# Turning attention probabilities with VectorE's 32x32 transposes and SBUF block copies instead of TensorE transposes

## The chip, the cores and the metric

The kernel runs on one core of one Trainium2 chip. The metric is the device time of one execution in microseconds (us). Of the kernel before, three timed runs and one profiled execution exist.

## The reference

Two layers of a diffusion backbone work on 512 latent tokens and 256 context tokens of width 1024, in fp32. Layer 0 is differential attention with 8 heads (two softmaxes per head, the second subtracted with a factor), layer 1 is grouped-query attention with 8 query heads and 2 key/value heads. Cut to what matters here:

```python
s = jnp.einsum('bqhgd,bkhd->bhgqk', qblk, k32) * scale
p = jax.nn.softmax(s, axis=-1)
out = jnp.einsum('bhgqk,bkhd->bqhgd', p, v)
# latent queries read 512 latent and 256 context keys in one softmax;
# context queries (layer 0 only) read the 256 context keys
o = o1 - lam * o2                      # layer 0
y = (o * silu(gate)) @ w_out           # then x + gate * rms_norm(y)
```

The order of the keys in the sum over k is free, as long as the probabilities and the value tokens have the same one.

## The kernel before, in words

Every product of two fp32 matrices is done as three products of fp32r parts (`mm3`, line 537): high by high, high by low, low by high. A "split" of a tile is therefore a ScalarE copy to the high part and a subtraction on VectorE or GpSimd for the low part. Weights come from HBM 512 KB at a time on SP's DMA queue into two `raw` buffers and are split into `whi` and `wlo` (`wsplit`, line 606).

**Attention.** A unit is one block of 128 queries of one head. TensorE writes its scores, 128 queries by 768 keys, into PSUM (`s_units`, line 1264, layer 0; `s1_units`, line 1849, layer 1). VectorE takes the row maximum, ScalarE the exponential with the row sum, VectorE the reciprocal, and GpSimd scales the row; in layer 0 a VectorE multiply-add joins the second softmax to the first. The probabilities p then stand with the queries on the partitions, but the product with the values needs the keys there. `tstep` (line 1346 and line 1879) turns them: for two units (256 queries) and two key blocks, four TensorE transposes of 128x128 against `ident` go into one PSUM bank `bk`, which is split into `ah` (ScalarE) and `al` (VectorE). `mstep` (line 1360 and line 1892) multiplies with the value tiles in `pv_mm` (line 542): six matmuls with 256 columns per step. Three such steps make up a pair of units with 768 keys. Context queries in layer 0 have one step, with 256 keys.

**Projections.** `proj_fm` makes queries, keys and gates with the weights as the stationary operand. The values are made with the tokens as the stationary operand: `v_mm` (line 1038, layer 0) and `proj_tok` (line 1560, layer 1) load 128 token columns of `hhi`/`hlo` (or `h1hi`/`h1lo`) and stream 256 weight columns. Six token tiles, eight k-blocks and three products make 144 matmuls for a pair of heads; layer 0 has four pairs, layer 1 one.

**What sets the order.** The program is recorded and put in order before it is emitted. `Step` and `flow` (lines 731 and 746) set the order of recording: a score step has a due time, a turning step comes `LA` = 7.0 units of TensorE work after its last score step, and the product `LM` = 4.5 after the turning step; projections fill in between (`piece`, line 711). `Plan.schedule` (line 290) then replays all instructions with prices of its own (`price`, line 238) on the five in-order queues, and whichever can start first goes first. At most eight DMAs are taken to be in flight. Its result is the order of the instructions on each engine; the hardware only waits on semaphores. `AB` is the number of buffers of `ah` and of `al`.

Of the kernel before, what the change touches and what calls it, by code (L numbers as in the profile page):

```python
# [15 lines left out]
P = 128  # L16
# [31 lines left out]
WBUFS = 3  # L48
XE = [2, 2, 2, 2, 3, 3]
# [24 lines left out]
AB = 3  # L74
MEM = 227168
AHEAD_OPS = 1500
MARGIN = 1.08
SLOT = {}
# [400 lines left out]
def tile_backbone(  # L479
# [56 lines left out]

    def mm3(o, ahi, alo, bhi, blo, start, stop):
# [4 lines left out]
    def pv_mm(o, vh, vl, c, ah, al, kt, first, last):  # L542
        terms = [(v, a, e) for v, a in ((vh, ah), (vl, ah), (vh, al)) for e in range(2)]
        for i, (v, a, e) in enumerate(terms):
            nc.tensor.matmul(o, v[:, kt + e, c], a[:, e * 256:e * 256 + 256], start=first and i == 0, stop=last and i == 5)
# [577 lines left out]
    with pl.pool("t0") as t0:  # L1123
# [58 lines left out]
        def qk_split_(h, rr, eng=nc.gpsimd):  # L1182
            qk[h] = tuple(t0.tile([P, T], F32R, tag=f"qk{i}", name=nm("qk"), bufs=1) for i in range(4))
            for r, hi, lo in ((rr[0], *qk[h][:2]), (rr[1], *qk[h][2:])):
                nc.scalar.copy(hi, r)
                eng.tensor_tensor(lo, r, f32(hi), ALU.subtract)
# [77 lines left out]
        def s_units(h, qts):  # L1264
            res = []

            def unit(qt):
                k0, nk = (0, T) if qt < NQ else (512, C)
                l, ps_ = small(2), []
                if nk == T:  # L1270
                    sc = [sc2(), sc2()]
                else:
                    if h < KT - 1 or qt == NQ:
                        sts["sc"] = sc2()
                    sc = [sts["sc"]] * 2
                w = 384 if nk == T else 256
                qh, ql, kh_, kl_ = qk[h]
                tok = slice(qt * P, (qt + 1) * P)
                prev = None
                for j in range(nk // w):  # L1280
                    c = slice(k0 + j * w, k0 + j * w + w)
                    for i, (a, b) in enumerate(((qh, kh_), (qh, kl_), (ql, kh_))):
                        for m in (1, 0):
                            r = slice(m * 64, m * 64 + 64)
                            with after(prev), chained(prev):
                                prev = nc.tensor.matmul(
                                    sc[m][:, j if nk == T else m, :w], a[r, tok], b[r, c], start=i == 0, stop=i == 2)
                for m in range(2):
                    scv = sc[m][:, :, :384] if nk == T else sc[m][:, m, :256]
                    mx = small()  # L1290
                    nc.vector.tensor_reduce(mx, scv, AX.XY if nk == T else AX.X, ALU.max, negate=True)
                    pt = t0.tile([P, T], F32, tag=f"p{m}", name=nm("p"), bufs=6 if m == 0 else 2)[:, :nk]
                    pv_ = pt.rearrange("p (j n) -> p j n", j=2) if nk == T else pt
                    nc.scalar.activation(pv_, scv, AF.Exp, bias=mx, accum_out=l[:, m:m + 1])
                    ps_.append(pt)
                    r = l[:, m:m + 1]
                    nc.vector.reciprocal(r, r)
                    if m == 0:
                        scaled(EP0, pt, pt, r)
                    else:  # L1300
                        nc.vector.tensor_tensor(r, r, nlam, ALU.mult)
                        nc.vector.scalar_tensor_tensor(ps_[0], pt, r, ps_[0], ALU.mult, ALU.add)
                        res.append(ps_[0])

            def unit_ctx():
# [3 lines left out]
                for qt in (NQ, NQ + 1):  # L1309
                    tok = slice(qt * P, (qt + 1) * P)  # L1310
                    for i, (a, b) in enumerate(((qh, kh_), (qh, kl_), (ql, kh_))):
                        for m in (1, 0):
                            r = slice(m * 64, m * 64 + 64)
                            with after(prev), chained(prev):
                                prev = nc.tensor.matmul(
                                    sc[m][:, qt - NQ, :C], a[r, tok], b[r, S:T], start=i == 0, stop=i == 2)
                l = [small(2), small(2)]
                pts = []
                for m in range(2):
                    mx = small(2)  # L1320
                    nc.vector.tensor_reduce(mx, sc[m][:, :, :C], AX.X, ALU.max, negate=True)
                    pt = t0.tile([P, T], F32, tag=f"p{m}", name=nm("p"), bufs=6 if m == 0 else 2)
# [19 lines left out]
        def pv_steps(h, at, ch, after, ts, ms):  # L1342
            kts = range(6) if ch < 2 else range(4, 6)
            st = {}

            def tstep(kt):
                tr = trp()
                for e in range(2):
                    j = kt + e - kts[0]
                    for i, a in enumerate(at):  # L1350
                        nc.tensor.transpose(tr[:, e * 256 + i * P:e * 256 + (i + 1) * P], a[:, j * P:(j + 1) * P], ident)
# [4 lines left out]
                nc.scalar.copy(ah, tr)  # L1356
                nc.vector.tensor_tensor(al, tr, f32(ah), ALU.subtract)
                st[kt] = ah, al

            def mstep(kt):  # L1360
# [6 lines left out]
                pv_mm(o, vh, vl, vc, ah, al, kt, kt == kts[0], kt == kts[-2])  # L1367
                if kt == kts[-2]:
# [5 lines left out]
                    nc.scalar.copy(gT[h][:, sl], o)  # L1374
# [185 lines left out]
    def proj_tok(o, w, t):  # L1560
        sl = slice(t * P, (t + 1) * P)
        for kt in range(KT):
            wh, wl = w[kt // 4]
            c = slice((kt % 4) * 256, (kt % 4) * 256 + 256)
            mm3(o, h1hi[:, kt, sl], h1lo[:, kt, sl], wh[:, c], wl[:, c], kt == 0, kt == KT - 1)
# [127 lines left out]
    with pl.pool("t1", "right") as t1p:  # L1693
# [45 lines left out]
        def k_tr(m, kr):  # L1739
# [4 lines left out]
            sl = slice(m * P, (m + 1) * P)  # L1744
            nc.scalar.copy(kh[:, :, sl], tv)
            nc.vector.tensor_tensor(kl[:, :, sl], tv, f32(kh[:, :, sl]), ALU.subtract)

        def k_rope(m, o, r):
            kn = t1p.tile([P, 256], F32, tag="qt", name=nm("kn"), bufs=10)
# [4 lines left out]
            if m < NQ:  # L1754
                kr = t1p.tile([P, 256], F32, tag="qt", name=nm("kr"), bufs=10)
# [6 lines left out]
        for what, m in KV:  # L1762
# [7 lines left out]
            else:  # L1770
# [3 lines left out]
                run(proj_tok(o, wk if what == "k" else wv, m))  # L1774
# [21 lines left out]
        def q_proj(p):  # L1796
# [4 lines left out]
            for m in range(NQ):  # L1801
# [3 lines left out]
                q = t1p.tile([P, 256], F32, tag="qt", name=nm("q"), bufs=10)  # L1805
# [43 lines left out]
        def s1_units(h, ms):  # L1849
            res = []  # L1850

            def unit(m):
# [4 lines left out]
                for j in range(2):  # L1857
                    c = slice(j * 384, j * 384 + 384)
                    mm3(sc[:, j, :384], qa[:, sl], qb[:, sl], kh[:, g, c], kl[:, g, c], True, True)
# [6 lines left out]
                pt = t1q.tile([P, T], F32, tag="p", name=nm("p"), bufs=5)  # L1866
                l = small()
                nc.scalar.activation(pt.rearrange("p (j n) -> p j n", j=2), scv, AF.Exp, scale=sr, bias=nmx, accum_out=l)
                nc.vector.reciprocal(l, l)
                scaled(EN1, pt, pt, l)  # L1870
                res.append(pt)
# [3 lines left out]
        def pv1_steps(h, at, ch, after, ts, ms):  # L1875
            g = h // 4
            st = {}

            def tstep(kt):
                tr = trp()  # L1880
                for e in range(2):
                    for i, a in enumerate(at):
                        nc.tensor.transpose(tr[:, e * 256 + i * P:e * 256 + (i + 1) * P], a[:, (kt + e) * P:(kt + e + 1) * P], ident)
# [4 lines left out]
                nc.scalar.copy(ah, tr)  # L1888
                nc.vector.tensor_tensor(al, tr, f32(ah), ALU.subtract)
                st[kt] = ah, al  # L1890

            def mstep(kt):
# [5 lines left out]
                pv_mm(o, vh, vl, c, ah, al, kt, kt == 0, kt == 4)  # L1898
                if kt == 4:
                    if ch == 0:  # L1900
                        gT1[h] = t1p.tile([P, 512], F32, tag="g1", name=nm("g1"), bufs=8)
                    (nc.scalar.copy if EG1 == "a" else nc.vector.tensor_copy)(gT1[h][:, ch * 256:ch * 256 + 256], o)
# [217 lines left out]
```

## Time and profile before

| | us |
|---|---|
| timed runs, median of 3 (lowest, highest) | 807.85 (807.48, 809.25) |
| the profiled execution, its own time | 808.79 |
| span from its first to its last instruction | 807.0 |
| TensorE busy | 786.4 |
| VectorE / ScalarE / GpSimd busy | 473.6 / 482.0 / 437.4 |

PE stands for TensorE's matmuls, PEld for its weight loads, DVE for VectorE, ACT for ScalarE, POOL for GpSimd, SP for the engine whose queue issues most DMAs; a trailing q (SPq, ACTq) is a sequencer. A row of a group gives engine, operation, output <- inputs, shape and count, then the busy time and the mean duration of one in ns, then the idle time ahead of them. A row of the timeline gives the start, the length, and what ran; neighbours of one kind are merged (x4). Matmuls overlap: each has a duration of 270 to 400 ns, and the next one starts long before that is over, so the distance between ends is what one costs. The recorder writes every instruction with line 395, so groups are told apart by tile names: in `bk<-ident,p` the moving operand is `ident` and the loaded one is p.

### The profile page before, as it was taken

The numbers are of one execution on the slowest core, as the hardware profiler recorded it, in microseconds if no ns is written. First come the engines' busy times: TensorE is split into PE (matmuls) and PEld (weight loads), VectorE is DVE, ScalarE is ACT, GpSimd is POOL, SyncE is SP. The second block draws the span as 40 slices with busy tenths as digits, with TensorE's granted clock in tenths as the row PEclk, the third lists the DMA queues.
The fourth block names the chain that finished last, engine by engine and source line by source line (L and its number), as shares of the span: only waits on it lengthen the run. The fifth ranks groups of instructions, "written<-read, shape, count | busy, mean of one in ns | idle before, by whom it ended". The sixth has DMA issues, their size and how long they took to land.

```text
span 807.0 us, 14385 instructions
## 1 busy us (share of the span) xinstructions
PE 786.4 (97%) x5482; PEld 699.8 (87%) x5482; DVE 473.6 (59%) x824; ACT 482.0 (60%) x1083; POOL 437.4 (54%) x512
## 2 busy tenths in 40 slices
PE   7899999999999999999999999999999999999997
PEld 5779888889887898797989998898999899898886
DVE  3425787774847546656546743788346455655625
ACT  5524577684565645666538843784466676768622
POOL 4545776874585654757923312366887646644101
PEclk9899999999999999999999999999999999999999
DMA  9951120132142431323430152035321200201112
GB/s 302 363 180 67 65 75 31 40 108 89 40 158 79 144 105 53 105 80 96 165 106 27 62 227 79 1 89 175 120 70 53 96 11 27 79 27 55 51 53 105
DMA packets 41541, 77.78 MB, mean 96 GB/s; under 512 B 3584, under 2 KB 18688, under 8 KB 41472
## 3 DMA queue, kind: packets, MB, share of 16 engines
q1 hardware_dynamic: 38048, 71.71, 27.4%
q10 hardware_dynamic: 3424, 5.15, 1.8%
q8 instruction: 43, 0.70, 0.4%
q14 instruction: 26, 0.21, 0.1%
HBM read 70.56 MB, written 2.10 MB: 90 GB/s over the span
## 4 chain that ended last, share of the span: by engine, by line
PE 91%; DVE 3%; ACT 2%; DMA 2%; issue 1%; SPq 0%; POOL 0%; ACTq 0%; DVEq 0%; POOLq 0%
PE bk L395 75%; PE sc L395 16%; DMA ag<-in_ada_w 1%; DMA raw<-in_post_g 1%; DVE gacc L395 1%; DMA gw<-in_ada_w 0%; ACT whi L395 0%; SPq L395 0%; DVE h L395 0%; ACT sq L395 0%; DVE hf L395 0%; ACT p L395 0%; DVE sw L395 0%; DVE gate L395 0%; ACT jk L395 0%
## 5 line engine op out<-in xcount | busy, mean ns | idle before, releaser
L395 PE MATMUL bk<-whi,h 128*128 128x256 f32 (+1 forms) x1184 | 244.6, 299 | 2.0 <-DVE kn L395 1.3
L395 PE MATMUL bk<-h,whi 128*128 128x512 f32 (+2 forms) x832 | 225.6, 351 | 0.0
L395 POOL TENSOR_TENSOR wlo<-raw,whi 128x256 fp32r<-128x256 f32 x200 | 162.5, 839 | 76.7 <-ACT whi L395 75.3
L395 PEld LDWEIGHTS bk<-whi,h 128*128 128x128 f32 x1184 | 191.0, 189 | 14.6 <-issue 4.9
L395 PE MATMUL bk<-wlo,h 128*128 128x256 f32 (+1 forms) x592 | 176.5, 299 | 0.0
L395 PEld LDWEIGHTS bk<-h,whi 128*128 128x128 f32 x832 | 144.1, 188 | 16.5 <-issue 4.4
L395 PE MATMUL bk<-h,wlo 128*128 128x512 f32 (+2 forms) x416 | 145.7, 351 | 0.0
L395 DVE TENSOR_REDUCE sm<-sc 128x1 f32<-128x768 f32 (+2 forms) x114 | 101.0, 897 | 25.7 <-PE sc L395 25.4
L395 PEld LDWEIGHTS bk<-wlo,h 128*128 128x128 f32 x592 | 111.7, 189 | 4.8 <-issue 1.4
L395 POOL TENSOR_SCALAR p<-p,sm 128x768 f32<-128x768 f32 (+1 forms) x80 | 68.4, 858 | 77.6 <-DVE sm L395 72.8
L395 DVE TENSOR_TENSOR al<-bk,ah 128x512 fp32r<-128x512 f32 x104 | 69.4, 685 | 39.3 <-ACT ah L395 38.8
L395 ACT CAST whi<-raw 128x1024 fp32r<-128x1024 f32 (+1 forms) x70 | 71.7, 1026 | 31.9 <-PE bk L395 27.7
L395 ACT ACTIVATE p<-sc,sm 128x768 f32<-128x768 f32 (+1 forms) x96 | 72.9, 762 | 21.6 <-DVE sm L395 15.6
L395 ACT CAST ah<-bk 128x512 fp32r<-128x512 f32 x104 | 59.0, 590 | 43.5 <-PE bk L395 43.1
L395 PEld LDWEIGHTS bk<-h,wlo 128*128 128x128 f32 x416 | 78.4, 188 | 7.5 <-issue 1.3
L395 PE MATMUL bk<-ident,p 128*128 128x128 f32 x416 | 64.3, 275 | 1.6 <-DVE ql L395 1.1
L395 PEld LDWEIGHTS bk<-ident,p 128*128 128x128 f32 x416 | 49.0, 141 | 11.4 <-issue 2.0
L395 DVE SCALAR_TENSOR_TENSOR p<-p,sm,p 128x768 f32<-128x768 f32 (+1 forms) x48 | 53.4, 1120 | 3.3 <-POOL p L395 0.5
L395 ACT ACTIVATE jk<-bk 128x128 f32<-128x128 f32 (+4 forms) x66 | 22.7, 345 | 53.5 <-PE bk L395 34.4
L395 POOL TENSOR_TENSOR sz<-sz,za 128x384 f32<-128x384 f32 (+1 forms) x24 | 29.4, 1227 | 40.3 <-ACT za L395 39.7
L395 PE MATMUL sc<-qk,qk 64*128 64x384 f32 (+1 forms) x480 | 50.6, 341 | 0.0
L395 DVE RECIPROCAL sm<-sm 128x1 f32<-128x1 f32 (+1 forms) x114 | 18.1, 159 | 52.0 <-ACT p L395 51.5
(191 smaller groups left out, 1375.5 us busy)
## 6 DMA issues: line engine op xcount, KB each, us to landing
raw<-in_a_w SPq DMA_DIRECT2D x30, 512.0 KB, 3.5
araw<-in_ada_w SPq DMA_DIRECT2D x12, 1024.0 KB, 5.3
raw<-in_b_w SPq DMA_DIRECT2D x20, 512.0 KB, 3.5
ag<-in_ada_w SPq DMA_DIRECT2D x32, 256.0 KB, 6.5
raw<-in_w_out SPq DMA_DIRECT2D x16, 512.0 KB, 3.6
sw<-qr ACTq DMA_DIRECT2D x32, 128.0 KB, 2.1
gw<-in_ada_w SPq DMA_DIRECT2D x8, 512.0 KB, 4.1
xt<-in_x SPq DMA_DIRECT2D x4, 512.0 KB, 5.1
```

The lines of the kernel that those rows point to most:

```text
L395: self.ops.append(getattr(eng, meth)(*args, **kw))
```

## The change

Two constants give the numbers of buffers; the parts of the new program that matter:

```diff
-AB = 3
+AB = 2
+P0B = 2
+ATB = 2
+PPB = 2
+PEWAY = ((), ())
```
```diff
+    def keys(src, t):
+        if t < NQ:
+            return src[:, :S].rearrange("p (x k) -> p k x", k=4)[:, t]
+        return src[:, S:].rearrange("p (x k) -> p k x", k=2)[:, t - NQ]
+
+    def ordered(t, r, lo, k):
+        a = by_a(t, 192)[:, :, :P] if k == 4 else by_a(t, 192)[:, :, P:]
+        return a.rearrange("p a (k j) -> p a k j", k=k), r.rearrange("p (a j k) -> p a k j", a=4, k=k)
+
+    def turn(pool, pp):
+        flat = pp.rearrange("p b u x -> p (b u x)")
+        nc.vector.transpose(flat, flat)
+        at = pool.tile([P, 4, 384], F32, tag="at", name=nm("at"), bufs=ATB)
+        for q in range(4):
+            for a in range(4):
+                nc.sync.dma_start(at[32 * a:32 * a + 32, q, :], flat[32 * q:32 * q + 32, a * 384:a * 384 + 384])
+        return at
+
+    def split_at(ah, al, src, moved):
+        hi, lo = (by_a(ah, P), by_a(al, P)) if moved else (ah, al)
+        nc.scalar.copy(hi, src)
+        nc.vector.tensor_tensor(lo, src, f32(hi), ALU.subtract)
```
```diff
     def v_mm(o, w, t, k_lo=0, k_hi=KT, first=True, last=True):
         for kt in range(k_lo, k_hi):
-            sl = slice(t * P, (t + 1) * P)
             c = slice((kt % 4) * 256, (kt % 4) * 256 + 256)
             wh, wl = w[kt // 4]
-            mm3(o, hhi[kt][:, sl], hlo[kt][:, sl], wh[:, c], wl[:, c], first and kt == 0, last and kt == KT - 1)
+            mm3(o, keys(hhi[kt], t), keys(hlo[kt], t), wh[:, c], wl[:, c], first and kt == 0, last and kt == KT - 1)
...
             def tstep(kt):
-                tr = trp()
...
+                if not moved:
+                    tr = trp()
...
-                nc.scalar.copy(ah, tr)
-                nc.vector.tensor_tensor(al, tr, f32(ah), ALU.subtract)
+                split_at(ah, al, at[0][:, :, kt * 64:kt * 64 + P] if moved else tr, moved)
```

With `PEWAY` empty, every pair of units with 768 keys is `moved`: 16 pairs in layer 0 and 16 in layer 1. Both units write their probabilities interleaved by blocks of 32 into one tile `pp` of 128x1536. One VectorE instruction transposes its 32x32 blocks in place. Sixteen DMAs on SP's queue, each of 32 partitions by 384 elements (48 KB), carry the blocks to the partitions where the product needs them, in a tile `at`. The three splits of the pair read `at` in SBUF, not a PSUM bank. The 12 TensorE transposes of a pair are no longer there. The context steps of layer 0 keep theirs.

A key's partition and block now follow from its number: token 4x+k of the latents stands in block k at partition x, token 2x+k of the context likewise. So `keys` gives the value projections every fourth token column (latents) or every second (context) as the stationary operand, in place of 128 neighbouring ones, and the key tiles are written in the matching order (`ordered` in `qk_split_`, and `k_tr`): the split of a head's keys in layer 0 becomes two copies and two subtractions in place of one each, and that of the two context tiles in layer 1 likewise. The copy that empties the product's bank puts the queries back in order. `qt` has 9 buffers, not 10.

The planner puts the instructions in a new order. Three places show it.

TensorE, layer 1, products of head 6, before (`ident,p` are transposes; `ah`, `al` the turned probabilities; `h`, `whi`, `wlo` a gate projection that fills in):

```order
L395 MATMUL bk_69<-h_689_5300,wlo_8000 128x512
L395 MATMUL bk_68<-ah_8536,vh 128x256 x2
L395 MATMUL bk_68<-ah_8536,vl 128x256 x2
L395 MATMUL bk_69<-h_689_5300,whi_7999 128x512
L395 MATMUL bk_71<-ident,p_8402 128x128
L395 MATMUL bk_71<-ident,p_8446 128x128
L395 MATMUL bk_71<-ident,p_8402 128x128
L395 MATMUL bk_71<-ident,p_8446 128x128
L395 MATMUL bk_68<-al_8537,vh 128x256 x2
L395 MATMUL bk_68<-ah_8570,vh 128x256 x2
```

The same stage in the change (`sc<-kh,qh` are scores of the next head):

```order
L399 MATMUL sc_73<-kh,qh_8460 128x384
L399 MATMUL bk_70<-al_8493,vh 128x256 x2
L399 MATMUL bk_70<-ah_8558,vh 128x256 x2
L399 MATMUL bk_70<-ah_8558,vl 128x256 x2
L399 MATMUL bk_70<-al_8559,vh 128x256 x2
L399 MATMUL sc_73<-kl,qh_8460 128x384
L399 MATMUL sc_73<-kh,ql_8461 128x384
L399 MATMUL bk_68<-h_690_5397,whi_8334 128x512
L399 MATMUL bk_70<-ah_8574,vh 128x256 x2
```

The transposes have gone from among the products, and nothing stands in their place.

VectorE, the same stage in the change (`pp` is the tile of a pair, `sm` row statistics, `h` and `g` parts of the gated output):

```order
L399 STREAM_TRANSPOSE pp_8588<-pp_8588 128x1536
L399 TENSOR_TENSOR al_8606<-at_8511,ah_8605 128x512
L399 TENSOR_TENSOR al_8652<-at_8511,ah_8651 128x512
L399 TENSOR_TENSOR h_1287_8935<-g_985_7276,h_1286_8934 128x512
L399 TENSOR_TENSOR al_8687<-at_8511,ah_8686 128x512
```

A transpose of 1536 columns has come in once per pair, and the low parts `al` are taken from `at` in place of `bk`.

SP's queue near the end of layer 1 in the change (`raw` are loads of weights):

```order
L399 DMA at_8294<-pp_8261 32x384 x16
L399 DMA raw_8658<-in_w_out 128x4x256
L399 DMA raw_8802<-in_w_out 128x2x512
L399 DMA at_8410<-pp_8374 32x384 x16
L399 DMA raw_8910<-in_w_out 128x2x512
L399 DMA at_8511<-pp_8478 32x384 x16
L399 DMA raw_9107<-in_w_out 128x2x512
L399 DMA at_8624<-pp_8588 32x384 x16
```

Before, only the loads stood there; now 16 block copies stand between them, and each queue entry waits behind the one ahead of it.

More of the change, by code (lines that the diff above doesn't have):

```diff
@@ L1344, in pv_steps @@
             st = {}
+            moved = ch < 2 and dma_way(0, h, ch)
             def tstep(kt):
-                tr = trp()
[L1348 to L1351, printed above, removed]
+                if not moved:
+                    tr = trp()
+                    for e in range(2):
+                        for i, a in enumerate(at):
+                            src = a[:, (kt + e - kts[0]) * P:(kt + e - kts[0] + 1) * P]
+                            nc.tensor.transpose(tr[:, e * 256 + i * P:e * 256 + (i + 1) * P], src, ident)
                 if h == 0 and ch == 0 and kt == 0:
@@ L1564, in proj_tok @@
             c = slice((kt % 4) * 256, (kt % 4) * 256 + 256)
[L1565 removed]
+            a, b = (keys(t_[:, kt, :], t) if perm else t_[:, kt, sl] for t_ in (h1hi, h1lo))
+            mm3(o, a, b, wh[:, c], wl[:, c], kt == 0, kt == KT - 1)
             yield 3 * 256 / 2400.0
@@ L1877, in pv1_steps @@
             st = {}
+            moved = dma_way(1, h, ch)
             def tstep(kt):
[L1880 to L1883, printed above, removed]
+                if not moved:
+                    tr = trp()
+                    for e in range(2):
+                        for i, a in enumerate(at):
+                            src = a[:, (kt + e) * P:(kt + e + 1) * P]
+                            nc.tensor.transpose(tr[:, e * 256 + i * P:e * 256 + (i + 1) * P], src, ident)
                 if h == 0 and ch == 0 and kt == 0:
@@ L1887, in tstep @@
                 al = t1q.tile([P, 512], F32R, tag="al", name=nm("al"), bufs=AB)
-                nc.scalar.copy(ah, tr)
-                nc.vector.tensor_tensor(al, tr, f32(ah), ALU.subtract)
+                split_at(ah, al, at[0][:, :, kt * 64:kt * 64 + P] if moved else tr, moved)
                 st[kt] = ah, al
```

134 lines of the change are left out of this document (99 added, 35 removed).

## Prediction

> **What bounds the kernel now.** I read the first part of the page, then its slices, then the chain.
>
> ```profile
> span 807.0 us, 14385 instructions
> PE 786.4 (97%) x5482; PEld 699.8 (87%) x5482; DVE 473.6 (59%) x824; ACT 482.0 (60%) x1083; POOL 437.4 (54%) x512
> PE   7899999999999999999999999999999999999997
> PE 91%; DVE 3%; ACT 2%; DMA 2%; issue 1%; SPq 0%; POOL 0%; ACTq 0%; DVEq 0%; POOLq 0%
> ```
>
> TensorE is idle for 807.0 - 786.4 = 20.6 us in all, mostly at the start. No other engine is busy for more than 60%. Two of the five stretches into which I cut the span hold nearly all the attention; the columns are from:to, sum, then PE, PEld, DVE, ACT and POOL busy, and the granted clock.
>
> ```profile
> 50.00:410.00 360.00, 359.36 (x2517) 310.02 (x2517) 228.08 (x363) 216.66 (x450) 231.83 (x228) 1.00 0.27 87
> 540.00:755.00 215.00, 209.28 (x1492) 196.88 (x1490) 120.99 (x241) 136.50 (x338) 133.27 (x170) 1.00 0.22 70
> ```
>
> In layer 0's attention (50 to 410 us) TensorE is idle for 0.6 us, in layer 1's (540 to 755) for 5.7, at the full granted clock, 1.00. So TensorE's instruction stream sets the time: what leaves it comes off the span in full, as long as its operands keep coming.
>
> **What the change removes.** 32 pairs of units, each with three turning steps of four transposes: 384 of the 416. Their price is not their mean duration, since matmuls overlap:
>
> ```profile
> 748.68 0.61 PE L395 MATMUL bk<-h,whi 128*128 128x512 f32 x2
> 749.14 0.40 PE L395 MATMUL bk<-h,wlo 128*128 128x512 f32 x1
> 749.37 0.62 PE L395 MATMUL bk<-h,whi 128*128 128x512 f32 x2
> ...
> 758.49 0.40 PE L395 MATMUL sc<-whi,h 128*128 128x256 f32 x2
> 758.73 0.28 PE L395 MATMUL sc<-wlo,h 128*128 128x256 f32 x1
> 758.85 0.60 PE L395 MATMUL bk<-ident,p 128*128 128x128 f32 x4
> 759.21 0.48 PE L395 MATMUL sc<-whi,h 128*128 128x256 f32 x2
> ...
> L395 PE MATMUL bk<-ident,p 128*128 128x128 f32 x416 | 64.3, 275 | 1.6 <-DVE ql L395 1.1
> ```
>
> From end to end: 512 columns cost (749.99 - 749.29)/3 = 0.233 us. For 256 columns the end at 758.89 is followed by one at 759.01: 0.12. The four transposes and two matmuls after that end at 759.69, so a transpose costs (759.69 - 759.01 - 2 x 0.12)/4 = 0.11, and 384 x 0.11 = **42.2 us** goes. A step of scores, 384 columns, is by proportion 0.175.
>
> **What it adds on the path: the way of one turn.** Until now p was consumed straight from SBUF. Now a pair goes through a VectorE transpose, 16 DMAs, and a split, while TensorE must find other work. Up to the last scaling the way stays as it is:
>
> ```profile
> 606.50 0.95 DVE L395 TENSOR_REDUCE sm<-sc 128x1 f32<-128x768 f32 x1
> 606.81 0.46 PEld L395 LDWEIGHTS bk<-ident,p 128*128 128x128 f32 x4
> ...
> 609.02 1.00 ACT L395 ACTIVATE p<-sc,sm,qrs 128x768 f32<-128x768 f32 x1
> ...
> 610.32 0.33 SPq L395 DMA_DIRECT2D raw<-in_b_w  x1
> ...
> 610.40 0.92 POOL L395 TENSOR_SCALAR p<-p,sm 128x768 f32<-128x768 f32 x1
> ```
>
> From 606.50 to 611.32 that is 4.8 us from the last score to scaled probabilities. The three unknown prices behind it have these nearest rows:
>
> ```profile
> L395 DVE TENSOR_TENSOR al<-bk,ah 128x512 fp32r<-128x512 f32 x104 | 69.4, 685 | 39.3 <-ACT ah L395 38.8
> L395 DVE TENSOR_REDUCE sm<-sc 128x1 f32<-128x768 f32 x96 | 90.3, 949 | 24.9 <-PE sc L395 24.6
> L395 DVE TENSOR_SCALAR xt<-xt,sm 128x1024 f32<-128x1024 f32 x5 | 4.2, 843 | 11.2 <-POOL sm L395 11.1
> L395 DVE TENSOR_TENSOR sw<-sw,rope 128x512 f32<-128x512 f32 x16 | 18.2, 1137 | 1.6 <-DMA sw<-qr 1.6
> ...
> L395 ACTq DMA_DIRECT2D sw<-qr x32: 472/560/885, 66.5 to 382.9; - x32
> ...
> raw<-in_b_w SPq DMA_DIRECT2D x20, 512.0 KB, 3.5
> sw<-qr ACTq DMA_DIRECT2D x32, 128.0 KB, 2.1
> ```
>
> - The transpose of 1536 columns. From 512 to 768 columns VectorE's time rises by 949 - 685 ns; 1024 more than 512 give 685 + 4 x 264 = 1.74 us. Bounds: 843 ns per 1024 (one SBUF input) make 1.26, 1137 per 512 make 3.4. I take **1.75**, near the reduction, which also has one input.
> - Issuing. One SP issue takes 0.33 us, an issue of `sw` (SBUF to SBUF, from ACT's queue) 0.56. Sixteen take **5.3** (up to 9.0), one queue in order. I take SP's row because these are SP's issues.
> - Landing. `sw` moves 128 KB in 2.1 us, `raw` 512 KB in 3.5. A copy is 48 KB; I take **2.1**, up to 3.5.
> - The split's first half, ScalarE's copy, is already there at 590 ns: 0.6.
>
> Together 4.8 + 1.75 + 5.3 + 2.1 + 0.6 = 14.6 us, with some queueing on VectorE and SP 15 to 17. The program gives TensorE the following work between the last score of a pair and its first product with the values, counted in its new order at 0.11, 0.12, 0.175 and 0.233 per matmul. The least is head 6's second pair: 36 matmuls of 256 columns, 31 of 512 and 18 of 384, that is 4.3 + 7.2 + 3.2 = 14.7 us. The other fifteen pairs of layer 1 have 15.8 to 23.4, half of them under 18. In layer 0 the first four have 17.9 to 20.6, the other twelve 31 to 66. So the way fits within the cover nearly everywhere, with stalls of one or two us at three or four pairs of layer 1: I put **5 us** in the sum. Bounds: 0 at the low prices (about 13 us against 14.7), 25 at the high ones (rival C).
>
> SP's queue is also shared. The copies stand between `raw` loads, and a load there mostly waits for its buffer:
>
> ```profile
> SPq L395 <- ACT whi L395: 194.5, 27, 20.9
> ...
> PE bk L395 <- DVE al L395: 1.8, 2, 1.4
> ```
>
> SP waits 194.5 us in 27 waits for the split that frees `raw`; copies queued behind such a load wait with it, and a load behind copies waits for the transpose. Behind a late load stand the weight split and, two loads later, a projection. TensorE hardly ever waits for `al` now (1.8 us in all); that line is the first that would grow.
>
> **What it adds beside the path.** VectorE: 32 x 1.75 = 56 us, and 96 `al` steps with both inputs in SBUF: the SBUF rows are `sw` above and this one,
>
> ```profile
> L395 DVE TENSOR_TENSOR h<-hf,h 128x512 fp32r<-128x512 f32 x20 | 15.7, 791 | 4.6 <-ACT h L395 4.0 <-POOL hf L395 0.6
> L395 ACT CAST h<-hf 128x512 fp32r<-128x512 f32 x12 | 7.3, 619 | 0.0
> L395 ACT CAST qk<-qr 128x768 fp32r<-128x768 f32 x16 | 13.1, 836 | 6.2 <-POOL qr L395 2.4 <-PE sc L395 2.2 <-DVE qr L395 1.5
> L395 POOL TENSOR_TENSOR qk<-qr,qk 128x768 fp32r<-128x768 f32 x14 | 27.5, 1972 | 6.9 <-ACT qk L395 6.0 <-PE bk L395 0.8
> ```
>
> 791 to 1137 against 685 ns, 10 to 44 us. So VectorE rises from 473.6 to 540 to 575 us of some 770, still below TensorE. `ah` from SBUF costs 619 against 590. The keys' split in two parts adds a second start on ScalarE and GpSimd per head; 836 and 1972 ns stay roughly what the whole costs, and GpSimd, busy for 54%, covers it. `AB` 2 instead of 3 makes the third split of a pair wait for the first one's products, 12 matmuls or 1.4 us; the split behind it takes about as long, so 0 to 0.8 us per pair where nothing else stands between, and it is inside the 5 us. If these covers went, the cost would show as TensorE's waits for `ah` or `al`.
>
> **The strided weight loads.** Value projections now load token columns that lie 16 bytes apart (latents) or 8 (context). Eight k-blocks times three products make 24 loads per token tile: 4 tiles x 5 projections x 24 = 480 at 16 bytes, 2 x 5 x 24 = 240 at 8. The row of these loads:
>
> ```profile
> L395 PEld LDWEIGHTS bk<-whi,h 128*128 128x128 f32 x1184 | 191.0, 189 | 14.6 <-issue 4.9
> ```
>
> No load of before is strided, so the cost is bounded: nothing, or what rival B has. The four loads at 606.81 step by (0.46 - 0.14)/3 = 0.107 us, with 141 ns for one of that kind; a matmul of 256 columns follows the last at 0.12. So loading is hidden now, but with only 0.01 us to spare. I take 0 because a TensorE load brings one column per 0.107/128 = 0.84 ns, while the moving side takes 0.233/512 = 0.46 ns per column of the same 4 bytes: loading asks the memory for half of what the engine gets from it elsewhere.
>
> [...]
>
> **The sum.** 808.8 (the profiled execution) - 42.2 + 5 = 771.6; the median shown lies 0.9 below the profiled execution, so **771 us** (A), between 764 and 778: with 0 of stalls 766, with 12 us 778, and 2 us less than 766 with 0.115 per transpose.
>
> **The rivals.**
> - B, slower: **the strided loads become the bound in the value projections**. At half speed, a load steps by 0.214 us in place of 0.107, and no longer hides behind a matmul of 0.118 to 0.12: +0.095 x 480 = 46 us, 771 + 46 = 817, with 810 where the stalls vanish because TensorE is later. With a price of 0.19, the whole duration of a load, 0.07 x 480 = 34 and 805; with 0.233, 55 and 826; if the 8-byte ones lose too, 23 more. It decides from 42.2/480 = 0.088 us more per load. For it: the spare of 0.01 us, and that nothing in the trace shows such a load as free. Against it: the half rate of loading above. I put it at 815 (800 to 826).
> - C, the **way of a turn is longer than its cover**: 0.56 us per issue, 3.5 landing and 3.4 for the transpose make 4.8 + 3.4 + 9.0 + 3.5 + 0.6 = 21.3 us against 14.7 to 23.4 in layer 1: a shortfall of 2 to 6 us at a dozen pairs, less what the first stall gives to the next, some 25 us: 766 + 25 = **791** (785 to 812 with loads held up on SP). For it: 16 copies per pair on one queue in order, SP's long waits. Against: in layer 0 the cover is 31 us and more at most pairs.
>
> [...]
>
> ```profile
> ccol<-in_c_col SPq DMA_DIRECT2D x1, 8.0 KB, 1.6
> out_x<-u SPq DMA_DIRECT2D x2, 128.0 KB, 1.8
> ```
>
> 8 KB take 1.6 us, 128 KB 1.8: nearly all of a 48 KB copy would be overhead, and that is already within the 2.1 us of the sum.
>
> **How the numbers follow.** A has a chance of 0.45, B 0.40, C 0.15. A measurement of this kernel can tell about 0.2%, or 1.6 us, from no change. A lies all on the faster side, C for most of its part (0.12); B is slower but for its lowest prices. So faster 0.57, same 0.03, slower 0.40. The range goes from A's low end, 764, to 822, and leaves out B's dearest part and mishaps beyond C; A's own is 764 to 778.
>
> **What will show it.** Right in A: TensorE's busy time falls from 786 to about 744, the waits of TensorE for `ah` and `al` stay under 8 us, the transpose takes 1.3 to 2.2 us, copies land in about 2 us, and the matmuls of the value projections still follow each other at 0.12 us. B shows as loads `bk<-whi,h` well above 189 ns on average and matmuls over 0.17 us apart in the value projections, while TensorE still counts as busy. C shows as idle time of TensorE ahead of `ah`/`al` matmuls, in layer 1 above all, released by ScalarE, behind that by the copies. The forecast is wrong if a copy's issue costs over 0.6 us, or if the planner's new order puts a load of weights that TensorE needs behind a turn.

## The result, and the profile after

The kernel with the change takes **937.27 us** (median of 4 runs, 935.2 to 939.0) against 807.66 (4 runs, 807.02 to 809.25) before: 1.16 times as long, 95% interval 1.1566 to 1.1635. The prediction was 771 us. One of the four runs of e1 below, 894.95 us, was in a slower state than the other three and is left out of its median.

The first part of the page, its PE and PEclk slices and its chain, after the change:

```profile
span 933.3 us, 14525 instructions
PE 838.5 (90%) x5098; PEld 742.2 (80%) x5098; DVE 524.4 (56%) x859; ACT 486.4 (52%) x1093; POOL 445.6 (48%) x519
...
PE   7999979999999799698998899999987967787887
PEclk8999999999999899798999999999998978998989
...
PE 53%; SPq 21%; DMA 7%; issue 5%; DVE 5%; ACT 5%; POOL 3%; ACTq 1%; DVEq 0%; POOLq 0%
```

The 384 transposes are gone (5482 to 5098 matmuls), and yet TensorE is busy 52 us longer. It is also idle for 933.3 - 838.5 = 94.8 us, 74 more than before, and SP's sequencer, nowhere to be seen before, holds 21% of the chain. So the slowdown has two faces: more busy time on TensorE, and more idle time.

The **busy time** first: the granted clock was full in some stretches and not in others, so a stretch at the full clock comes first. These are stretches by time, with the columns of the prediction's:

```profile
610.00:690.00 80.00, 78.25 (x523) 76.12 (x521) 39.88 (x99) 36.15 (x113) 53.38 (x74) 1.00 0.33 102
690.00:770.00 80.00, 62.10 (x363) 56.31 (x363) 43.76 (x68) 41.72 (x97) 37.28 (x50) 0.87 0.37 104
770.00:850.00 80.00, 63.98 (x330) 55.74 (x329) 48.41 (x69) 45.16 (x96) 36.14 (x41) 0.89 0.38 101
```

In the first stretch stand the value projections of layer 1. TensorE's timeline there, first at latent tokens (every fourth column), then at context tokens (every second):

```profile
612.58 0.63 PE L399 MATMUL bk<-whi,h 128*128 128x256 f32 x2
613.05 0.39 PE L399 MATMUL bk<-wlo,h 128*128 128x256 f32 x1
613.28 0.63 PE L399 MATMUL bk<-whi,h 128*128 128x256 f32 x2
...
642.14 0.41 PE L399 MATMUL bk<-whi,h 128*128 128x256 f32 x2
642.38 0.28 PE L399 MATMUL bk<-wlo,h 128*128 128x256 f32 x1
642.50 0.41 PE L399 MATMUL bk<-whi,h 128*128 128x256 f32 x2
```

From the end at 613.21 to the end at 613.91 three matmuls of 256 columns take 0.70 us, 0.233 each; at the context tokens three take 642.91 - 642.55 = 0.36, 0.12 each, as before. At the full clock, then, a load of columns 16 bytes apart doubles the step, and one of columns 8 bytes apart does not. The mean of the loads in the page says the same:

```profile
L399 PEld LDWEIGHTS bk<-whi,h 128*128 128x128 f32 x1184 | 233.3, 229 | 15.9 <-issue 5.1
```

189 ns before, 229 now. In the other two stretches TensorE is idle for 17.9 and 16.0 of 80 us and the granted clock is 0.87 and 0.89, against 1.8 and 1.00 in the first: each wait seems to be paid a second time, by slower work around it (e1 and e4 below compare the same matmuls).

The **idle time**: the waits, then SP's timeline in layer 1, then the rows of the new operations.

```profile
PE bk L399 <- ACT ah L399: 50.1, 17, 6.5
PE bk L399 <- DMA araw<-in_ada_w: 11.9, 2, 7.8
...
ACT ah L399 <- DMA at<-pp: 74.6, 22, 5.8
...
SPq L399 <- DVE pp L399: 77.0, 15, 9.4
```

```profile
790.00 10.02 SPq L399 DMA_DIRECT2D at<-pp  x16
800.11 0.53 SPq L399 DMA_DIRECT2D raw<-in_b_w  x1
800.74 0.39 SPq L399 DMA_DIRECT2D raw<-in_w_out  x1
801.49 21.16 SPq L399 DMA_DIRECT2D at<-pp  x32
```

```profile
at<-pp SPq DMA_DIRECT2D x512, 48.0 KB, 1.9
...
L399 DVE STREAM_TRANSPOSE pp<-pp 128x1536 f32<-128x1536 f32 x32 | 56.7, 1772 | 9.9 <-POOL pp L399 9.9
...
L399 ACT CAST ah<-at 128x512 fp32r<-128x512 f32 x96 | 57.4, 617 | 99.0 <-DMA at<-pp 74.6
...
L399 DVE TENSOR_TENSOR al<-at,ah 128x512 fp32r<-128x512 f32 x96 | 76.2, 814 | 85.2 <-ACT ah L399 79.8
```

The transpose takes 1.77 us, the landing 1.9, the splits 0.62 and 0.81: as forecast. Issuing does not: sixteen issues take at least 10.0 us (10.0 to 11.5 in the rows of this trace), 0.63 us each at best, where the sum had 0.33. TensorE waits for `ah`, `ah` for the copies, and the copies stand one behind the other in SP's queue. That is the picture of layer 1: of the 50.1 us only 8.3 fall into layer 0's attention. There the longest wait, 11.9 us, is for `araw`, a load of weights that goes through the same queue and for which TensorE did not wait before; the prediction had named such a load among the signs of being wrong.

### The profile page after: what moved, and what is told of

Its sections match the earlier page's. It is cut to its first block, busy times and chain, and to the rows that moved or that the text cites. A ratio compares the mean times of both kernels' runs of the same rounds, so it can differ in the third digit from the quotient of the medians.

```text
span 933.3 us, 14525 instructions
## 1 busy us (share of the span) xinstructions
PE 838.5 (90%) x5098; PEld 742.2 (80%) x5098; DVE 524.4 (56%) x859; ACT 486.4 (52%) x1093; POOL 445.6 (48%) x519
## 4 chain that ended last, share of the span: by engine, by line
PE 53%; SPq 21%; DMA 7%; issue 5%; DVE 5%; ACT 5%; POOL 3%; ACTq 1%; DVEq 0%; POOLq 0%
PE bk L399 45%; SPq L399 21%; PE sc L399 8%; DMA at<-pp 3%; DVE pp L399 2%; ACT ah L399 1%; DMA raw<-in_a_w 1%; DMA araw<-in_ada_w 1%; POOL pp L399 1%; DVE sm L399 1%; DVE h L399 1%; DMA raw<-in_w_out 1%; DMA raw<-in_b_w 1%; DVE hf L399 1%; POOL qr L399 1%
## 5 line engine op out<-in xcount | busy, mean ns | idle before, releaser
L399 PE MATMUL bk<-whi,h 128*128 128x256 f32 (+1 forms) x1184 | 289.1, 331 | 2.5 <-DVE tb L399 1.0
L399 PEld LDWEIGHTS bk<-whi,h 128*128 128x128 f32 x1184 | 233.3, 229 | 15.9 <-issue 5.1
L399 PEld LDWEIGHTS bk<-wlo,h 128*128 128x128 f32 x592 | 135.4, 229 | 5.0 <-issue 1.9
L399 POOL TENSOR_SCALAR pp<-pp,sm 128x768 f32<-128x768 f32 x64 | 62.6, 979 | 137.3 <-DVE sm L399 98.7
L399 DVE TENSOR_TENSOR al<-at,ah 128x512 fp32r<-128x512 f32 x96 | 76.2, 814 | 85.2 <-ACT ah L399 79.8
L399 ACT CAST ah<-at 128x512 fp32r<-128x512 f32 x96 | 57.4, 617 | 99.0 <-DMA at<-pp 74.6
L399 PE MATMUL bk<-ah,vh 128*128 128x256 f32 x96 | 25.7, 357 | 42.0 <-ACT ah L399 41.9
L399 DVE STREAM_TRANSPOSE pp<-pp 128x1536 f32<-128x1536 f32 x32 | 56.7, 1772 | 9.9 <-POOL pp L399 9.9
L399 PEld LDWEIGHTS sc<-qk,qk 64*128 64x128 f32 x480 | 39.0, 188 | 15.8 <-issue 5.2
L399 ACT ACTIVATE p<-sc,sm 128x768 f32<-128x768 f32 (+1 forms) x64 | 43.9, 689 | 9.7 <-DVE sm L399 6.5
```

The source lines that it names most:

```text
L399: self.ops.append(getattr(eng, meth)(*args, **kw))
```

## The experiments

Times are medians, beside runs of the kernel before of the same series (medians between 807.5 and 808.5).

**Strided loads alone.** The kernel before, with the change's operand in the value projections (layer 0 is shown, layer 1's `proj_tok` likewise):

```diff
-            mm3(o, hhi[kt][:, sl], hlo[kt][:, sl], wh[:, c], wl[:, c], first and kt == 0, last and kt == KT - 1)
+            mm3(o, keys(hhi[kt], t), keys(hlo[kt], t), wh[:, c], wl[:, c], first and kt == 0, last and kt == KT - 1)
```

> The kernel before with one edit: the value projections load every fourth (latents) or every second (context) token column, as in the change; the value tokens are then not in the order of the probabilities, so the attention's output is another one. Theory (a load at 16 bytes of distance takes twice as long, at 8 bytes it does not): 480 x 0.111 = 53 us more, 808 to 861 (855 to 866), loads of 320 ns in place of 189 for 480 of them. Rival 1 (both distances are slow): 720 x 0.111 = 80 us, 888. Rival 2 (the slow loads of the change come from its DMAs or its lower granted clock): 808 to 812.

Measured 860.54 us (859.79 to 862.13), ratio 1.0658 (1.0634 to 1.0683): 53.0 us more, to the microsecond 480 x 0.111. The page:

```profile
span 859.2 us, 14385 instructions
PE 841.2 (98%) x5482; PEld 754.7 (88%) x5482; DVE 467.7 (54%) x824; ACT 481.7 (56%) x1083; POOL 436.1 (51%) x512
...
PE   7999999999999999999999999999999999999997
...
L395 PEld LDWEIGHTS bk<-whi,h 128*128 128x128 f32 x1184 | 232.0, 228 | 13.2 <-issue 4.9
```

The same number of instructions on every engine, no new DMA, 18.0 us of idle time against 20.6 before, and the loads' mean at 228 ns as in the change: all of it is the load. The other way round, the change with keys and tokens stored by blocks (the key tiles are written in the same order, not shown):

```diff
     def keys(src, t):
-        if t < NQ:
-            return src[:, :S].rearrange("p (x k) -> p k x", k=4)[:, t]
-        return src[:, S:].rearrange("p (x k) -> p k x", k=2)[:, t - NQ]
+        return src[:, t * P:(t + 1) * P]
```

> The change, but keys and value tokens are stored by blocks (token 128k+x in block k at partition x), so that no weight load is strided and the keys' split is one copy again; the 16 copies per pair stay. Theory (two separate losses, strided loads and SP's queue): the 480 loads of 0.229 us go back to 0.118, TensorE's busy time falls by 53 us from 838 to about 785, and the time from 937 to about 885 (875 to 900). Rival (SP's queue alone sets the time, and the slow loads only fill its gaps): busy falls as much, but idle grows by it, and the time stays above 920.

Measured 882.56 us (881.64 to 885.95, 3 runs), ratio 1.094 (1.0907 to 1.0972): 54.7 less than the change.

```profile
span 879.5 us, 14523 instructions
PE 784.9 (89%) x5098; PEld 687.8 (78%) x5098; DVE 526.6 (60%) x857; ACT 481.5 (55%) x1091; POOL 449.9 (51%) x519
...
PE bk L399 <- ACT ah L399: 47.3, 18, 5.9
```

Busy time falls from 838.5 to 784.9, idle time stays at 94.6. Strides and stalls are separate losses, and a layout without strides was to be had: the order of the keys is free, so each group of 32 keys can be any 32 neighbours.

**The number of issues.** From here on keys are stored by blocks. First four copies in place of sixteen:

```diff
         for q in range(4):
-            for a in range(4):
-                nc.sync.dma_start(at[32 * a:32 * a + 32, q, :], flat[32 * q:32 * q + 32, a * 384:a * 384 + 384])
+            nc.sync.dma_start(at[:, q, :], flat[:, q * 384:q * 384 + 384])
```

> As e1_block_keys, with 4 copies of 128x384 per pair in place of 16 of 32x384: the same bytes, but each copy stays on its partitions, so the blocks of 32 are not moved across and the attention's output is another one. Theory (number of issues on SP): 4 x 0.59 = 2.4 us per turn in place of 9.4, the way of a turn is about 11.5 us and fits under the cover; idle time of TensorE near the 21 us of before, time 768 to 785. Rival (buffers, or the bytes through the DMA engines): as e1 within 10 us.

Measured 783.64 us (782.26 to 784.85), ratio 0.9704 (0.9684 to 0.9724): 98.9 us under e1 with the same bytes. Page, then the issues:

```profile
span 781.0 us, 13982 instructions
PE 749.1 (96%) x5098; PEld 661.8 (85%) x5098; DVE 538.6 (69%) x857; ACT 480.8 (62%) x1091; POOL 457.0 (59%) x519
...
at<-pp SPq DMA_DIRECT2D x128, 192.0 KB, 2.3
```

192 KB land in 2.3 us, 48 KB in 1.9, and an issue takes 0.60 us here and 0.59 in e1 (medians): the price is per copy at these two sizes. Two buffers alone don't stall TensorE, for they are the same here. TensorE's busy time is 36 us lower than in e1 with the same matmuls, while the mean granted clock rises from 0.947 to 0.995: the lower clock explains that difference (784.9 x 0.947 and 749.1 x 0.995 are 743 and 745). This version leaves out the move across partitions, so it only measures a price.

Then half of the sixteen from ScalarE's queue:

```diff
-                nc.sync.dma_start(at[32 * a:32 * a + 32, q, :], flat[32 * q:32 * q + 32, a * 384:a * 384 + 384])
+                (nc.scalar if q % 2 else nc.sync).dma_start(at[32 * a:32 * a + 32, q, :], flat[32 * q:32 * q + 32, a * 384:a * 384 + 384])
```

> As e1_block_keys, with half of the 16 copies of a pair issued from ScalarE's queue. Theory (16 issues of 0.59 us, 9.4 us on SP's queue in order, make the way of a turn longer than its cover): the way gets 4.7 us shorter, though ScalarE loses 0.56 x 256 = 143 us to issuing; TensorE's idle time falls well below that of e1, time 820 to 860. Rival (the stalls come from the fewer buffers, AB, pp and at): as e1 within 10 us, or slower by ScalarE's issues.

Measured 891.78 us (890.23 to 893.64), ratio 1.1045 (1.102 to 1.1069): the theory's number fell. The rival's number held (9.2 us over e1), but not its mechanism, the buffers, as the waits show. TensorE's and ScalarE's waits, then ScalarE's timeline:

```profile
PE sc L399 <- ACT pp L399: 28.0, 11, 5.4
...
PE bk L399 <- ACT ah L399: 6.6, 3, 4.8
...
ACT sm L399 <- DMA at<-pp: 53.6, 12, 7.6
```

```profile
747.34 3.20 ACTq L399 DMA_DIRECT2D at<-pp  x4
750.59 0.37 ACT L399 COPY g<-bk 128x256 f32<-128x256 f32 x1 [3.50 <-PE bk L399]
750.61 2.50 ACTq L399 DMA_DIRECT2D at<-pp  x4
753.16 0.59 ACT L399 CAST qh<-bk 128x512 fp32r<-128x512 f32 x1 [2.20 <-DMA at<-pp]
```

TensorE's wait for `ah` did shrink, from 47.3 us in e1 to 6.6. A new one took its place: the issues now stand before ScalarE's exponentials and copies, and TensorE waits for score banks to come free.

**The planner's price.** `Plan.schedule` counts 330 ns for an issue on SP. One line:

```diff
-                go = s + (330 if e == "SP" else 450)
+                go = s + (590 if op.cost == 49152 else 330 if e == "SP" else 450)
```

> As e1_block_keys, but the planner counts 590 ns for the issue of a 48 KB copy, as measured in the change, in place of 330, and so orders the program for it. Theory (SP's queue is too slow in itself: 16 issues make 9.4 us per pair, and layer 1 has a pair every 11 us where nothing stalls, with loads of weights besides): little is gained, 865 to 884. Rival (the stalls come from an order planned with the wrong price, and TensorE has other work to put there): under 850.

Measured 816.71 us (813.29 to 821.46), ratio 1.011 (1.0059 to 1.0162): 65.9 us under e1. **My theory fell, the rival held.** Stretches of the layers' attention (e1, then e5), from the first scores to the last products:

```profile
79.00:491.00 412.00, 377.36 (x2512) 325.55 (x2512) 271.73 (x415) 240.03 (x515) 239.11 (x234) 0.95 0.37 112
615.00:845.00 230.00, 184.35 (x1074) 166.63 (x1074) 129.33 (x201) 126.97 (x284) 103.24 (x126) 0.90 0.35 97
```

```profile
81.00:456.00 375.00, 365.24 (x2518) 317.69 (x2517) 279.20 (x415) 240.19 (x514) 243.29 (x233) 0.99 0.40 123
580.00:787.00 207.00, 180.61 (x1086) 162.59 (x1084) 132.41 (x200) 126.41 (x284) 105.32 (x126) 0.93 0.39 108
```

In layer 0 the idle time falls from 34.6 us to 9.8, in layer 1 from 45.6 to 26.4. TensorE's wait for `ah` falls from 47.3 us in all to 13.5, that for `araw` from 11.3 to 2.1. The same copies, the same queue, another order of instructions: with the short price TensorE's stream, which runs in the planned order, came to products whose operands were not there yet, with other work behind them. The same line in the change itself, with its strides:

> The change with one edit: the planner counts 590 ns for the issue of a 48 KB copy in place of 330; the strided loads stay. Theory (order planned with a wrong price, and strided loads, are two losses that add): 937 - 67, as e1 to e5, = 870 (860 to 880). Rival (with the loads slow, TensorE's slower stream already covers part of the waits): the gain is under 50 us, 890 or more.

Measured 871.13 us (870.07 to 874.75), ratio 1.0788 (1.0756 to 1.0819): 66.1 us under the change, as much as from e1 to e5 without the strides. The two losses add. With half of the issues on ScalarE's queue and 600 ns on both:

```diff
-                go = s + (330 if e == "SP" else 450)
+                go = s + (600 if op.cost == 49152 else 330 if e == "SP" else 450)
```

> As e3_two_queues (half of the copies from ScalarE's queue), but the planner counts 600 ns for the issue of a 48 KB copy on either queue. Theory (e3's loss, too, came from issues planned too short, and with the right price half the issues on another queue relieve SP): under e5's 817, 795 to 812. Rival (issues on ScalarE stand before exponentials and copies that TensorE waits for, whatever the order): 817 to 850.

Measured 877.41 us (874.5 to 881.3), ratio 1.0861 (1.0817 to 1.0906): 14 under e3, but 61 over e5, and above the numbers of both theory and rival. Of the two the rival's mechanism fits: TensorE still waits 30.6 us for score banks that ScalarE's exponentials free (28.0 in e3). On ScalarE's queue the issues stay dear even when they are planned.

**By layers.** With the right price, layer 1 turned by TensorE:

```diff
-PEWAY = ((), ())
+PEWAY = ((), ((0, 0), (0, 1), (1, 0), (1, 1), (2, 0), (2, 1), (3, 0), (3, 1), (4, 0), (4, 1), (5, 0), (5, 1), (6, 0), (6, 1), (7, 0), (7, 1)))
```

> As e5_issue_price, with the pairs of layer 1 turned by TensorE as before, so 16 turns by copies in layer 0 and 256 copies. Theory (in layer 0 the 16 issues per pair hold up loads of weights on SP's queue, 45 us in e1's trace against e4's between the first scores and the last products): 192 transposes save 21 us, some 30 to 45 come back as waits for weights, 807 - 21 + 38 = 824 (812 to 835). Rival (with a cover of 31 us and more layer 0 loses nothing by its turns): 787 to 795.

Measured 799.08 us (796.85 to 800.04), ratio 0.9886 (0.9859 to 0.9913): between the two, and **faster than before**, by 9.4 us of the 21.1 that 192 transposes make. The loss in layer 0 that the theory feared was mostly the price's. And layer 0 by TensorE except its first pair:

```diff
-PEWAY = ((), ())
+PEWAY = (((0, 1), (1, 0), (1, 1), (2, 0), (2, 1), (3, 0), (3, 1), (4, 0), (4, 1), (5, 0), (5, 1), (6, 0), (6, 1), (7, 0), (7, 1)), ())
```

> As e5_issue_price, with all pairs of layer 0 but the first turned by TensorE: 17 turns by copies, 16 of them in layer 1. Theory (the way of a turn in layer 1 is longer than its cover, 55 us in e1's trace against e4's from the first scores to the last products): 204 transposes save 22 us, 807 - 22 + 55 = 840 (825 to 845). Rival (the stalls of layer 1 are carried over from layer 0's late loads): 790 to 800.

Measured 844.19 us (843.59 to 844.52), ratio 1.0445 (1.0429 to 1.0462): on the theory's number, though above e5 with all 32 turns, which the theory doesn't explain. The layers do not simply add once the order changes. Then every second pair of layer 1, with all of layer 0:

```diff
-PEWAY = ((), ())
+PEWAY = ((), ((0, 1), (1, 1), (2, 1), (3, 1), (4, 1), (5, 1), (6, 1), (7, 1)))
```

> As e5_issue_price, with the first pair of each head of layer 1 turned by TensorE: 24 turns, and in layer 1 one turn for every 22 us. Theory (layer 1 loses where SP's queue has 9.4 us of issues per 11 us; at half that rate the way fits): 96 more transposes saved than in e6, 10.6 us, and up to 5 back, 799 - 10.6 + 3 = 791 (786 to 798). Rival (each turn of layer 1 costs more than its 1.3 us, whatever the rate): 803 or more, on the way from e6's 799 to e5's 817.

(As the diff shows, it is the second pair of each head that TensorE turns here and in e15 and e17, not the first, as the text above has it; the count is the same.)

Measured 823.93 us (821.65 to 829.97), ratio 1.0207 (1.0159 to 1.0255): above the theory and above e5 too, so half the rate on SP is no cheaper. That speaks against SP's throughput as the limit.

**What is left in layer 1.** First a closer price (in the rows above, issues follow each other every 0.63 us) for all turns and for e10's:

```diff
-                go = s + (590 if op.cost == 49152 else 330 if e == "SP" else 450)
+                go = s + (640 if op.cost == 49152 else 330 if e == "SP" else 450)
```

> As e5_issue_price with 640 ns in place of 590: in the traces the issues of one turn follow each other every 0.633 us, 0.589 for one and 0.044 between. Theory (what is left of the loss is an order still planned a little short, 16 x 0.044 = 0.7 us per turn): 800 to 812. Rival (the loss left in layer 1 is SP's throughput or the few buffers, and the order can't help): 814 to 820.

> As e10_half_layer1 (layer 0 and every second pair of layer 1 by copies) with the price 640. Theory (order planned short): 790 to 805. Rival (a turn in layer 1 costs TensorE more than it saves, by its long way with two buffers): 815 or more, again above e6's 799.

Measured 816.0 us (814.04 to 819.24), ratio 1.0101 (1.0075 to 1.0127), and 822.21 (820.76 to 825.45), ratio 1.0168 (1.0147 to 1.019): both within the rivals' numbers, no more to gain from the price. A longer planned lead in layer 1, in e13's kernel:

```diff
-LA = (7.0, 7.0)
+LA = (7.0, 10.0)
```

> As e13_price_640, with LA of layer 1 at 10.0 in place of 7.0, so that the recorded order puts the splits 3 us of TensorE work later behind the scores. Theory (the cover between scores and products is too short in layer 1): 5 to 15 us under e13. Rival (the planner orders by its prices, and the buffers bound the lead): e13 within 4, or slower.

Measured 813.03 us (808.33 to 816.3), ratio 1.0063 (1.0042 to 1.0083): 3.0 under e13, within the rival's bound. Longer leads weren't tried, nor a third buffer of `ah` and `al` beside copies in layer 1. Last, e15 with four straight copies per turn in layer 1 alone (`short`; the planner counts 640 ns for each of these, too):

```diff
+            if short:
+                nc.sync.dma_start(at[:, q, :], flat[:, q * 384:q * 384 + 384])
-            for a in range(4):
+            for a in range(0 if short else 4):
```

> As e15_half_640 (layer 0 and every second pair of layer 1 by copies), but in layer 1 a turn has 4 copies of 128x384 that stay on their partitions, in place of 16 of 32x384: the blocks aren't moved across, so layer 1's attention has another output. Theory (a turn of layer 1 is dear by the length of its way, 16 issues in one queue, which is longer than the work that the buffers allow ahead): 10.1 us of issues become 2.5 per turn, and the time falls from 822 to 785 to 798, under e14's 798. Rival (the transpose, the splits from SBUF or the order that the planner finds are dear whatever the copies take): 812 or more.

Measured 787.07 us (786.29 to 788.48), ratio 0.9747 (0.9726 to 0.9767): 35 us under e15 for eight turns. The timeline of one turn of each, e15 and then e17:

```profile
658.14 1.77 DVE L399 STREAM_TRANSPOSE pp<-pp 128x1536 f32<-128x1536 f32 x1
659.94 10.73 SPq L399 DMA_DIRECT2D at<-pp  x16
672.17 1.14 ACT L399 CAST ah<-at 128x512 fp32r<-128x512 f32 x2 [3.32 <-DMA at<-pp]
```

```profile
664.32 1.77 DVE L399 STREAM_TRANSPOSE pp<-pp 128x1536 f32<-128x1536 f32 x1
666.11 2.45 SPq L399 DMA_DIRECT2D at<-pp  x4
672.31 1.16 ACT L399 CAST ah<-at 128x512 fp32r<-128x512 f32 x2
```

And the stretch from the first scores of layer 1 to its last products, in e15 and in e17:

```profile
577.00:783.00 206.00, 182.03 (x1146) 166.93 (x1145) 112.55 (x191) 127.73 (x281) 100.13 (x127) 0.93 0.27 77
```

```profile
577.00:745.00 168.00, 165.14 (x1130) 154.03 (x1129) 117.59 (x190) 123.97 (x279) 105.27 (x125) 1.00 0.28 92
```

From the end of the transpose to the first split lie 672.17 - 659.91 = 12.3 us in e15, the last 3.3 of them with ScalarE waiting for the copies; in e17 it is 672.31 - 666.09 = 6.2, with the four issues over after 2.5 and ScalarE busy with other work before the split. TensorE's wait for `ah` in the stretch falls from 16.0 us to 0.8, its idle time from 24.0 to 2.9, and its clock rises from 0.93 to 1.00. So what makes a turn of layer 1 dear is its sixteen issues and the way that they lengthen, not the transpose or the splits. (Fewer issues also leave SP's queue freer and give the planner another order; this run doesn't tell these apart.)

**The version that gains.** Copies in layer 0, TensorE in layer 1, the price 640, and three buffers of `ah` and `al` in layer 1 (for `al` likewise):

```diff
-            if len(ms) >= AB:
-                t.lag.append((ms[-AB], 0.0))
+            if len(ms) >= AB + layer:
+                t.lag.append((ms[-AB - layer], 0.0))
...
-                ah = t1q.tile([P, 512], F32R, tag="ah", name=nm("ah"), bufs=AB)
+                ah = t1q.tile([P, 512], F32R, tag="ah", name=nm("ah"), bufs=AB + 1)
```

> As e6_layer0_only (copies in layer 0 alone, TensorE's transposes in layer 1) with the price 640, and three buffers of ah and al in layer 1 as before the change. Theory: the version that gains: 799 or a little less, 790 to 800. Rival (fewer buffers cost nothing in layer 1 and the price is right enough): 799 within 2.

Measured 798.11 us (796.32 to 800.26, 5 runs), ratio 0.9882 (0.9861 to 0.9903): 1.2% faster than before, and no different from e6. The third buffer and the finer price bring nothing that shows here. Two questions have no time on record: turning by copies only the second pair of each head in layer 0, and the kernel before with two buffers in place of three and nothing else.

## Why the prediction was wrong, point by point

- **Removed transposes, 42.2 us.** Right as far as shown: in e4, where little stalls, TensorE is busy 749.1 us, 37.3 less than before (the forecast said about 744); e17 saves 288 of them, 31.7 us by the sum, and comes out 21 under its before, with layer 0's longer way still in it.
- **The strided loads, taken at 0.** This step failed. I argued from the rate of the moving side that a load had spare bandwidth; a mean over contiguous columns says nothing of columns 16 bytes apart. Rival B's price, 0.095 us more per load and 46 us in all, was near: it measured 0.111 and 53.0. Its half speed was an estimate of mine that no run showed then. What the change's trace shows is a step of 0.233 us at 16 bytes of distance and of 0.12, as before, at 8.
- **Sixteen issues, 5.3 us.** This step failed too. I took SP's row for loads from HBM (0.33), while the row of the same kind of transfer, `sw` from SBUF to SBUF, had 0.56. It measured 0.59, 0.63 with the gap, so 10.0 us and more, above even the bound of 9.0. All the other terms of the way held: 1.77 for the transpose against 1.75, 1.9 for the landing against 2.1, 0.62 for the split.
- **Stalls of 5 us, at most 25.** The largest miss: the idle time rose by 74 us, and the lower clock cost some 41 more by an estimate from these runs (838.5 - 786.4 + 42.2 - 53.0; the 797.2 us that are left without them at the 0.993 of before would be 838 at the 0.945 of the change). Two things failed here. I set the longer way against the work *counted* between scores and products, and left out that this order had been planned with 0.33 per issue: what the wrong price did to TensorE's stream was 66 us (e1 to e5, the change to e9). And I did not price the clock, which was lower where TensorE stalled: 0.90 in layer 1's attention in e1, with 45.6 us of idle time, against 1.00 before, with 5.7.
- **Layer 0's cover of 31 us and more.** It did not protect layer 0, which had 34.6 us of idle time in e1; with the right price 9.8. The cover was counted for the products alone, while the longest wait there was for a load in the shared queue (`araw`, 11.3 us in e1).
- **The rivals as alternatives.** B and C each had a chance of their own, and none for both at once. Both happened, and they added: 54.7 for the strides (the change to e1); 65.9 for the price (e1 to e5); 33.1 from e5 to e4 for the number of issues (roughly, since e4 is planned with the old price); 17.9 from e4 to 765.7, where the sum without stalls stood. 765.7 + 17.9 + 33.1 + 65.9 + 54.7 = 937.3. These are steps from one run to the next, so that they end at the measured time is no test. The test is that two of them come out the same from another start: the strides 53.0 in e2, the price 66.1 in e9.
- **`AB` from 3 to 2, and VectorE.** Small: e14's third buffer in layer 1 gains nothing that shows, and e4 and e17 keep two buffers. Whether a third one would let copies in layer 1 run further ahead was not tried. VectorE is busy 524 us, below the forecast 540 to 575.
- **The idle time before.** The 20.6 us were not mostly at the start: the first 50 us hold 7.2 of them. Nothing in the sum hangs on it.

Still open: the last 17.9 us. In e4's profile TensorE is idle for 31.9 us, 11.3 more than before, and busy 4.9 more than 744.2. e17, with half the turns in layer 1 and all of layer 0's at sixteen copies, still stands 10.7 over its own sum (808.1 - 31.7 = 776.4). Which waits carry it was not tried apart. Open, too, is why e7 is slower than e5.

## What to carry to other kernels

Price a new operation by the row nearest in *kind*, a copy from SBUF to SBUF by such a copy, and give its price to whatever plans the order before judging the change: here one line of the planner was worth 66 us. Work that is taken off the engine that bounds the kernel pays only if the way around it is covered by other work of that engine; e14 keeps the way around where it is (layer 0) and gains 1.2%, while e5, with copies in layer 1 too, loses 1.1%. And when a layout is free, choose the one whose reads are contiguous on the engine that bounds: here that was worth 54.7 us (the change to e1).

## What the runs showed of the hardware

- A load of 128 fp32r columns 16 bytes apart costs a step of 0.233 us with 256-column matmuls (the change), where 8 bytes apart (the change) or contiguous (before) it hides at 0.12; 480 of them, with 240 loads 8 bytes apart beside them, cost 53.0 us (e2).
- An issue of a copy from SBUF to SBUF occupies SP's queue for about 0.6 us whether it moves 48 KB (0.59, e1) or 192 KB (0.60, e4): four straight ones take 2.45 us (e17), sixteen of 32 partitions 10.0 to 11.5 (the change).
- A stall of TensorE is paid twice here: with the same matmuls its busy time was 784.9 us at a mean granted clock of 0.947 (e1) and 749.1 at 0.995 (e4).
